# A hybrid encoder layer: output projection in 512-column products over four PSUM banks, the first half's MLP block sums kept in SBUF, and the attention mask moved from TensorE into the scan

## The chip, the cores and the metric

The kernel runs on one core of a Trainium2 chip, in one launch. The core has TensorE (products and transposes, into PSUM), VectorE, ScalarE, GpSimd and SyncE; here SyncE issues the loads from DRAM and GpSimd the stores. The metric is the device time of one execution in microseconds, as the median of several runs. One more run was recorded by the profiler, and every row below is from it.

## The reference

One layer over 2048 tokens of width 1024, in float32:

```
h    = rmsnorm(x, norm_mix_g) * (1 + sc_m) + sh_m
proj = h @ w_in                       # q, k, v, conv gates, gating MLP
z    = (q @ k.T) / 8                  # 8 heads of 64, keys s strictly before query t
w    = where(mask, exp(log_sigmoid(z) + sum over s<j<t of log_sigmoid(-z_j)), 0)
a    = w @ v
mix  = concat[a, short_gated_conv, spatial_gating] @ w_out
x    = x + g_m * mix
h    = rmsnorm(x, norm_mlp_g) * (1 + sc_f) + sh_f
x    = x + g_f * (square(relu(h @ mlp_w1)) @ mlp_w2)
out  = rmsnorm(x, final_norm_g)
```

## The kernel before

The tokens are cut into two halves of 1024, each half into two groups of 512 (`gl`), each group into four token blocks of 128 (`tb`). Every large product is made in float32r from a high and a low part of both operands, in three passes (`PASSES`): a contraction of 1024 takes eight slices of 128 times three passes, 24 instructions, into one PSUM bank. `split` makes the two parts with a ScalarE copy (L127) and a VectorE subtraction (L130).

`run` (L865) goes through four segments of blocks of units: the projections and attention of half 0 and of half 1, then the output projection of half 0 and of half 1. A unit is a piece of weights (`Unit`: loaded, split, held in `wtile`s) with a function that uses it. `bg.tick()` calls between the products step generators in the background: attention tasks, input preparation, modulation sums. The order of instructions on each engine is fixed when the kernel is built, by a list scheduler, and each engine works its own list in order.

An attention task (`attention`, L445) covers 256 queries of one head, each block of 128 against its own key block and the one before. It makes `z` with two products per block, and adds a mask of -1e38 in a third product, the identity times `mask` (L459), so that masked keys vanish. `weights` (L432) then makes log-sigmoids on ScalarE (L434 to L436), sums them backwards over keys with a scan on VectorE (L440), subtracts (L442) and exponentiates (L443). Two ticks later the weights `e` are transposed on TensorE into `wt` (L467), copied back, and one tick later multiplied with the values into `av` (L479). Keys further back are treated in `far_keys` only if a flag says so; every engine reads that flag and branches (L680, L681).

In the output projection (`out_unit`, L751) a unit holds 256 columns of `w_out`. For each pair of token blocks it loads the residual `xr`, makes 48 products of 256 columns into one bank `po` (L278, in `tok_major`), multiplies by the gate (L769, reading PSUM), adds `xr` (L771) and stores to `x1d`. While half 1 is in this segment, `prepare_input(0)` (L971) works in the background on half 0: it loads rows of `x1d`, takes squares on ScalarE, scales the rows on VectorE (L987), transposes them (L992) into banks of the common pool `pp`, and stores the result to `hd`. It then loads `hd` back, makes four block sums for a Strassen-like product with seven sub-products (L1011 to L1014) and stores them to `hs`. `inputs_after` (L1040) loads all seven inputs back (`hr`) and splits them into `h` tiles, which are shared with the projection's input `hT`, and `hx` tiles.

`Up.run` (L1073) makes 224 groups of 12 products with 512 columns into banks `pa`, `pb`, `pc`; `Down.run` (L1205) makes the second MLP product with 512 columns into banks `py`.

Of the kernel before, what the change touches and what calls it, by code (L numbers as in the profile page):

```python
# [84 lines left out]
def trunk(ctx: ExitStack, tc: tile.TileContext, x, c, ada_w, ada_b, norm_mix_g, norm_mlp_g,  # L85
# [49 lines left out]
    class Unit:  # L135


        def __init__(self, pieces):
            self.pieces, self.raw, self.w = pieces, None, None
# [10 lines left out]
        def ready(self):  # L150
            if self.w is None:
                self.fetch()
                self.w = []
                for j in range(2):
                    w = wtile()
                    split(w[:, 0], w[:, 1], self.raw[j], A)
                    w = w.rearrange("p s (k n) -> p s k n", n=UC)
                    self.w += [w[:, :, k] for k in range(KT // 2)]
            return self.w

    def unit_cols(wd, *starts):
# [8 lines left out]
        return Unit(pieces)  # L170

# [138 lines left out]
    with ExitStack() as ph:  # L310
# [86 lines left out]
        identb = ac.tile([P, P], BF16, name="identb")  # L397
        mask = ac.tile([P, 256], BF16, name="mask")
# [4 lines left out]
        def mixer_constants():  # L403

            V.tensor_copy(identb, ident)
            m32 = etile("m32")[:, :256]
            GP.memset(m32, 0.0)
            GP.affine_select(out=m32[:, P:], in_=m32[:, P:], pattern=[[-1, P]],
                             compare_op=ALU.is_gt, fill=NEG, base=0, channel_multiplier=1)
            GP.memset(m32[:, 0:P], NEG)  # L410
            V.tensor_copy(mask, m32)
# [20 lines left out]
        def weights(e, z, lo, init, save):  # L432
# [5 lines left out]
            for a, b in lo:  # L438
                r = e[:, a:b][:, ::-1]
                V.tensor_tensor_scan(r, r, r, init, ALU.add, ALU.bypass)  # L440
            V.tensor_copy(save, e.rearrange("p (b k) -> p b k", b=len(lo))[:, :, 0])
            V.tensor_tensor(e, z, e, ALU.subtract)  # L442
            A.activation(e, e, AF.Exp)  # L443

        def attention(half, pair, j, gl, qp, qq, kk, vv, a_sb):  # L445
# [5 lines left out]
            last = None  # L451
            for b in range(2):
                o = (2 * qp + b) * P
                c0 = 256 * b if first and b == 0 else 256 * b + P
                zb = z[:, b * 256:(b + 1) * 256]
# [6 lines left out]
            weights(e, z, ((0, 256), (256, G)), 0.0, carry[:, half, h, ib:ib + 2])  # L462
# [288 lines left out]
        def out_unit(half, n):  # L751
            cl = slice(n * UC, (n + 1) * UC)

            def run(gl, w):
                g = half * NG + gl
                gate = gate_bc[:, cl].unsqueeze(1).to_broadcast([P, 2, UC])
                for tb in range(0, 4, 2):
                    t0 = tb * P
                    xr = etile("xr")
                    load(out=xr.rearrange("p (b n) -> p b n", b=2),  # L760
                         in_=x2[g * G + t0:g * G + t0 + 2 * P, cl].rearrange("(b p) n -> p b n", p=P))
                    ps = bank("po")
                    for b in range(2):
                        tok_major(ps[:, b * UC:(b + 1) * UC], w, hT[gl], tb + b)
                        if half == 1:
                            bg.tick()
                            bg.tick()
                    t = etile("mo")
                    V.tensor_tensor(t.rearrange("p (b n) -> p b n", b=2),  # L769
                                    ps.rearrange("p (b n) -> p b n", b=2), gate, ALU.mult)  # L770
                    V.tensor_tensor(t, t, xr, ALU.add)  # L771
                    store(out=x1d[g][t0:t0 + 2 * P, cl].rearrange("(b p) n -> p b n", p=P),
                          in_=t.rearrange("p (b n) -> p b n", b=2))
                    bg.tick()
            return run

        def out_blocks(half):
            us = [(unit_cols(w_out2, n * UC), out_unit(half, n)) for n in range(D // UC)]
            return [us[0:2], us[2:4]]
# [85 lines left out]
        def run(seg, coming):  # L865

            for bn, blk in enumerate(blocks[seg]):
                last = bn == len(blocks[seg]) - 1
                for gl in range(NG):
# [5 lines left out]
                    for unit, use in blk:  # L875
# [8 lines left out]
                        if seg in (1, 2) and bn == 1 and gl == 0 and unit is blk[0][0]:  # L884
                            bg.drain()
                            far_keys(seg - 1, flags[seg - 1])
# [27 lines left out]
    class Up:  # L914
# [55 lines left out]

        def prepare_input(self, half):  # L971

            for g in range(NG):
                for tp in range(2):
                    xs = []
                    ss = sp.tile([P, 4], F32, name="ss", tag="ss")
                    for b in range(2):
                        t0 = (2 * tp + b) * P
                        t = landing("x")
                        load(out=t, in_=x1d[half * NG + g][t0:t0 + P, :])  # L980
                        xs.append(t)
                    yield
                    for b in range(2):
                        sum_squares(ss[:, b:b + 1], xs[b])
                    r = rstd_of(ss[:, 0:2], 2, 1.0 / D)
                    for b in range(2):
                        V.tensor_scalar_mul(xs[b], xs[b], r[:, b:b + 1])  # L987
                    yield
                    for k in range(0, KT, 2):
                        pt = bank("pt")  # L990
                        for m in range(4):
                            T.transpose(pt[:, m * P:(m + 1) * P],  # L992
                                        xs[m % 2][:, (k + m // 2) * P:(k + m // 2 + 1) * P], ident)
                        f = etile("hf")
                        for m in range(2):
                            sl = slice(m * UC, (m + 1) * UC)
                            A.activation(f[:, sl], pt[:, sl], AF.Identity,
                                         bias=SH_F[:, k + m:k + m + 1], scale=SC_F[:, k + m:k + m + 1])
                        t0 = g * G + tp * UC
                        store(out=hd[half][k:k + 2, :, t0:t0 + UC].rearrange("k p t -> p k t"),  # L1000
                              in_=f.rearrange("p (k t) -> p k t", k=2))
# [16 lines left out]
        def input(self, half, i):  # L1018

            tiles = []  # L1020
            for j in range(2):
# [10 lines left out]
                if i < 4:  # L1032
                    t = htile(2 * i + j)
                else:
                    t = self.xp.tile([P, 2, 2, G], F32R, name="hx", tag=f"hx{2 * i + j}")
                split(t[:, 0], t[:, 1], raw, A)
                tiles.append(t)
            self.h[half][i] = tiles

        def inputs_after(self, gl):  # L1040

            if gl == 0:
                bg.finish(self.coming)
                for i in (4, 5, 6, 0, 1):
                    self.input(0, i)
            else:
# [295 lines left out]
```

## Time and profile before

| | |
|---|---|
| three runs, median (lowest to highest) | 2219.91 us (2218.26 to 2220.62) |
| profiled execution: time, span of its records | 2221.83 us, 2220.1 us |
| TensorE busy; instructions | 2129.2 us (96%); 11071 |
| VectorE busy; instructions | 1445.0 us (65%); 2413 |
| ScalarE busy; instructions | 1013.7 us (46%); 1718 |
| granted TensorE clock, mean | 0.985 of full speed |
| DRAM read, written | 262.18 MB, 142.67 MB |
| stages, from the first instruction of each: attention, output projection, MLP up, MLP down | 0, 713.5, 941.8, 1600.0 us |

Busy time of TensorE counts from the start of a product to its modelled end; neighbours overlap, so a mean duration is longer than the distance between two starts, and prices of products are taken from such distances. [...]

### The profile page before, as it was taken

What the parts mean: (1) busy time and instruction counts of PE and PEld (TensorE: products, weight loads), DVE (VectorE), ACT (ScalarE), POOL (GpSimd) and SP (SyncE); (2) the same over time, 40 slices, a digit from 0 to 9 for tenths busy, and PEclk for the clock granted to TensorE, in tenths of its full rate; (3) what the DMA queues carried; (4) which work ended last, traced back from release to release, by engine and by line L of the source; (5) the groups of instructions that cost most, each with busy time, mean ns of one, the idle gap of its engine ahead of it and who ended that gap; (6) DMA issues with size and microseconds to landing.
All of it is one profiled execution on the core that took longest, in us unless ns stands there. A gap on an engine that the chain in (4) does not pass through costs nothing. (4 is left out here: it accounts for less than half of the span.)

```text
span 2220.1 us, 30066 instructions
## 1 busy us (share of the span) xinstructions
PE 2129.2 (96%) x11071; PEld 1797.7 (81%) x11071; DVE 1445.0 (65%) x2413; ACT 1013.7 (46%) x1718; POOL 332.0 (15%) x579
## 2 busy tenths in 40 slices
PE   7999999999999988899999999999999999999998
PEld 3887887888788988877888777878788888888886
DVE  4878868767768543776766777778743434347675
ACT  4645647645656234366444644444523323224432
POOL 0021211020211112223322132323200000000000
PEclk9999999999999999999999999999999999999999
DMA  8464544243435466967744687777854435437572
GB/s 304 134 207 115 163 142 131 68 140 88 117 121 162 135 224 233 327 225 244 280 156 154 225 280 256 253 237 248 308 188 153 159 120 165 143 126 231 199 241 86
DMA packets 223216, 415.37 MB, mean 187 GB/s; under 512 B 18400, under 2 KB 106416, under 8 KB 223056
## 3 DMA queue, kind: packets, MB, share of 16 engines
q1 hardware_dynamic: 177424, 264.28, 36.9%
q0 software_dynamic: 45504, 149.00, 19.3%
q8 instruction: 90, 1.47, 0.3%
q14 instruction: 70, 0.57, 0.1%
q10 hardware_dynamic: 128, 0.04, 0.0%
HBM read 262.18 MB, written 142.67 MB: 182 GB/s over the span
## 5 line engine op out<-in xcount | busy, mean ns | idle before, releaser
L1201 PE MATMUL py<-h,w 128*128 128x512 f32 x2688 | 610.7, 389 | 0.0
L1201 PEld LDWEIGHTS py<-h,w 128*128 128x128 f32 x2688 | 504.5, 188 | 105.8 <-issue 1.0
L130 DVE TENSOR_TENSOR w<-ar,w 128x1024 fp32r<-128x1024 f32 x112 | 137.1, 1224 | 263.7 <-ACT w L127 263.3
L127 ACT CAST w<-ar 128x1024 fp32r<-128x1024 f32 x112 | 118.0, 1054 | 370.4 <-PE py L1201 350.4
L127 ACT CAST w<-raw 128x512 fp32r<-128x512 f32 (+1 forms) x215 | 155.1, 736 | 131.4 <-PE pc L1089 48.9
L278 PE MATMUL po<-w,h 128*128 128x256 f32 x1536 | 195.0, 289 | 9.9 <-DVE mo L769 7.3
L130 DVE TENSOR_TENSOR w<-raw,w 128x512 fp32r<-128x512 f32 (+1 forms) x215 | 176.8, 834 | 37.9 <-ACT w L127 36.9
L278 PEld LDWEIGHTS po<-w,h 128*128 128x128 f32 x1536 | 191.4, 197 | 10.7 <-issue 10.0
L1089 PE MATMUL pc<-hx,w 128*128 128x512 f32 x768 | 193.2, 401 | 6.8 <-DVE hid L1063 6.8
L1089 PE MATMUL pa<-h,w 128*128 128x512 f32 x768 | 190.0, 396 | 7.8 <-ACT s L1056 7.8
L1089 PE MATMUL pb<-h,w 128*128 128x512 f32 x768 | 186.7, 391 | 3.6 <-DVE s L1058 3.6
L1089 PEld LDWEIGHTS pc<-hx,w 128*128 128x128 f32 x768 | 145.7, 190 | 42.6 <-DVE hid L1063 8.1
L1089 PEld LDWEIGHTS pa<-h,w 128*128 128x128 f32 x768 | 145.7, 191 | 42.4 <-ACT s L1056 11.2
L1089 PEld LDWEIGHTS pb<-h,w 128*128 128x128 f32 x768 | 143.8, 188 | 35.1 <-DVE s L1058 3.7
L269 PE MATMUL pc<-h,w 128*128 128x512 f32 x576 | 137.4, 394 | 0.0
L269 PEld LDWEIGHTS pc<-h,w 128*128 128x128 f32 x576 | 106.6, 188 | 21.3
L1064 ACT ACTIVATE hid<-hid 128x512 f32<-128x512 f32 x96 | 60.5, 630 | 124.2 <-DVE hid L1063 123.1
L278 PE MATMUL pv<-w,h 128*128 128x256 f32 x768 | 99.5, 285 | 0.0
L1300 POOL DMA_DIRECT2D out_dram<-y x24 | 13.0, 541 | 560.8 <-DVE y L1299 559.6
L1089 PE MATMUL pb<-hx,w 128*128 128x512 f32 x384 | 95.1, 396 | 1.2 <-DVE s L1058 1.2
L278 PEld LDWEIGHTS pv<-w,h 128*128 128x128 f32 x768 | 94.5, 191 | 0.1
L269 PE MATMUL pk<-h,w 128*128 128x512 f32 x384 | 94.1, 398 | 0.1
(215 smaller groups left out, 3285.3 us busy)
## 6 DMA issues: line engine op xcount, KB each, us to landing
ar<-ad SPq DMA_DIRECT2D x112, 512.0 KB, 3.9
ad<-hid POOLq DMA_DIRECT2D x128, 256.0 KB, 3.2
raw<-in_mlp_w_dram SPq DMA_DIRECT2D x62, 512.0 KB, 5.7
ad<-hsum POOLq DMA_DIRECT2D x96, 256.0 KB, 3.2
aw<-in_ada_w_dram SPq DMA_DIRECT2D x32, 512.0 KB, 4.5
f<-in_mlp_w_dram SPq DMA_DIRECT2D x32, 512.0 KB, 4.7
w2s<-f POOLq DMA_DIRECT2D x64, 256.0 KB, 2.9
w<-w2s SPq DMA_DIRECT2D x32, 512.0 KB, 4.5
```

The lines of the kernel that those rows point to most:

```text
L127: A.copy(hi, src)
L130: V.tensor_tensor(lo, src, hi.bitcast(F32), ALU.subtract)
L269: T.matmul(ps, lhsT=w[k][:, a, c0:c0 + P], rhs=hT[k][:, b], start=n == 0, stop=n == 3 * KT - 1)
L278: T.matmul(ps, lhsT=hT[k][:, a, tb * P:(tb + 1) * P], rhs=w[k][:, b], start=n == 0, stop=n == 3 * KT - 1)
L1064: A.activation(t, t, AF.Relu)
L1089: T.matmul(ps[key], lhsT=w[:, a, k * P:(k + 1) * P], rhs=h[k // 2][:, b, k % 2], start=start and m == 0, stop=m == 11, skip_group_check=no ...
L1201: T.matmul(ps[tb], lhsT=self.a[q][:, a, u * G + tb * P:u * G + (tb + 1) * P], rhs=self.w[at, c][:, b, u], start=c == 0 and u == 0 and n == ...
L1300: (load if end else store)(out=out2[t0:t0 + P, sl], in_=y)
```

## The change

- Output projection: a unit now holds 512 columns for half of the contraction (`unit_block`). `OutUnit` opens four `po` banks, one for each token block, runs 12 products of 512 columns into each with the first half of the weights, then 12 more with the second half, and after each of these the gate product, the addition and the store. `xr` is loaded one token block ahead. There is a tick after every 12 products (two or three in half 1).
- Attention: `mask`, `identb` and their products go. The scan multiplies its running value with `restart`, which is 0 on the diagonal and 1 elsewhere, so the sum begins anew there; after the subtraction a `min` with `cap` (-1e38 for masked keys, 0 elsewhere) works on the own block.
- First half's MLP inputs: `prepare_first` transposes through a bank of its own (tag `t`), keeps the four results of a column pair in SBUF, makes the sums there and splits three of them straight into `hx` tiles. Only what the other four inputs need goes through DRAM; these are loaded ahead and split later (`first_inputs`, and in `Up.run` at n = 1 and 3). There are more steps between load, squares, scaling and transposes (`rows_T`, used for half 1 too).
- The far-key branch of half 1 stands one unit earlier; inputs of half 1 load one step ahead; the first weights of the down stage follow the new places of the tiles.

```diff
             for a, b in lo:
                 r = e[:, a:b][:, ::-1]
-                V.tensor_tensor_scan(r, r, r, init, ALU.add, ALU.bypass)
+                if own is None:
+                    V.tensor_tensor_scan(r, r, r, init, ALU.add, ALU.bypass)
+                else:
+                    V.tensor_tensor_scan(r, r, restart[:, ::-1], init, ALU.add, ALU.mult)
             V.tensor_copy(save, e.rearrange("p (b k) -> p b k", b=len(lo))[:, :, 0])
             V.tensor_tensor(e, z, e, ALU.subtract)
+            if own is not None:
+                V.tensor_tensor(own, own, cap.unsqueeze(1).to_broadcast([P, 2, P]), ALU.min)
             A.activation(e, e, AF.Exp)
...
-                with tc.issue_after(last.ins) if last is not None else nullcontext():
-                    T.matmul(zb, lhsT=qq[:, 0, o:o + P], rhs=kk[:, o:o + 256], start=True, stop=False)
-                    T.matmul(zb, lhsT=qq[:, 1, o:o + P], rhs=kk[:, o:o + 256], start=False, stop=False)
-                    last = T.matmul(z[:, c0:(b + 1) * 256], lhsT=identb, rhs=mask[:, c0 - 256 * b:256],
-                                    start=False, stop=True)
+                for s in range(2):
+                    T.matmul(z[:, b * 256:(b + 1) * 256], lhsT=qq[:, s, o:o + P],
+                             rhs=kk[:, o:o + 256], start=s == 0, stop=s == 1)
...
+            def part(self, kh):
+                def run(gl, w):
+                    g = self.half * NG + gl
+                    if kh == 0:
+                        self.ps = [bank("po") for tb in range(4)]
+                    for tb in range(4):
+                        t0 = tb * P
+                        if kh == 1 or tb == 3:
+                            xr = self.xr
+                            if 4 * kh + tb < 7:
+                                t1 = g * G + (tb + 1) % 4 * P
+                                self.xr = etile("xr")
+                                load(out=self.xr, in_=x2[t1:t1 + P, self.cl])
+                        n = 12 * kh
+                        for k in range(KT // 2):
+                            for a, b in PASSES:
+                                T.matmul(self.ps[tb], lhsT=hT[gl][4 * kh + k][:, a, t0:t0 + P],
+                                         rhs=w[k][:, b], start=n == 0, stop=n == 23)
+                                n += 1
+                        if kh == 1:
+                            t = etile("mo")
+                            V.tensor_tensor(t, self.ps[tb], gate_bc[:, self.cl], ALU.mult)
+                            V.tensor_tensor(t, t, xr, ALU.add)
+                            store(out=x1d[g][t0:t0 + P, self.cl], in_=t)
+                        bg.tick()
+                        if self.half == 1:
                             bg.tick()
+                            if tb % 2:
+                                bg.tick()
...
+        def rows_T(self, half, g, tp, order, tile_, bank_):
...
+                load(out=t, in_=x1d[half * NG + g][t0:t0 + P, :])
+                xs.append(t)
+            yield None
+            yield None
+            for b in range(2):
+                sum_squares(ss[:, b:b + 1], xs[b])
+            yield None
+            r = rstd_of(ss[:, 0:2], 2, 1.0 / D)
+            for b in range(2):
+                V.tensor_scalar_mul(xs[b], xs[b], r[:, b:b + 1])
+            yield None
+            yield None
+            for k in order:
+                pt = bank_("pt")
...
+        def sums_first(self, tp, k, kept):
+            a11, a12, a21, a22 = kept[0, k], kept[0, k + 4], kept[1, k], kept[1, k + 4]
+            s1, s2, s4 = (self.xp.tile([P, G], F32, name="s", tag="s", bufs=3) for _ in range(3))
+            V.tensor_tensor(s1, a21, a22, ALU.add)
+            V.tensor_tensor(a21, a11, a21, ALU.subtract)
+            V.tensor_tensor(s2, s1, a11, ALU.subtract)
+            V.tensor_tensor(s4, a12, s2, ALU.subtract)
...
+            for i, t in ((1, s2), (3, a21), (4, s1)):
+                yield
+                o = self.h[0][i][k // 2]
+                split(o[:, 0, :, cols_], o[:, 1, :, cols_], t.rearrange("p (k t) -> p k t", k=2), A)
```

How this moves instructions shows at three places. TensorE's list where attention ends and the output projection begins, before (one tick's worth: the values' product `av` and the transposes `wt` of two older tasks, `z` of a new one):

```order
L278 MATMUL po<-w,h_7287 128x256 x6
L479 MATMUL av<-wT,vt 128x256 x2
L479 MATMUL av<-wT,vt 128x128 x4
L467 MATMUL wt<-ident,e 128x128 x4
L457 MATMUL z<-kk,qq 128x256
L458 MATMUL z<-kk,qq 128x256
L459 LDWEIGHTS identb
L459 MATMUL z<-mask,identb 128x128
L457 MATMUL z<-kk,qq 128x256
L458 MATMUL z<-kk,qq 128x256
L459 LDWEIGHTS identb
L459 MATMUL z<-mask,identb 128x128
```

and the same place after the change:

```order
L469 MATMUL z<-kk,qq 128x256 x4
L786 MATMUL po<-w,h_7224 128x512 x6
L786 MATMUL po<-w,h_7225 128x512 x6
L490 MATMUL av<-wT,vt 128x256 x2
L490 MATMUL av<-wT,vt 128x128 x4
L478 MATMUL wt<-ident,e 128x128 x4
L469 MATMUL z<-kk,qq 128x256 x4
```

The mask products are gone, and between one tick's pieces and the next stand 12 products of 512 columns in place of 48 of 256; the transposes `wt` of a task come two such groups after its `z`, here as before.

TensorE's list at the start of the output projection of half 1, before, where `pt` are the transposes of half 0's MLP input:

```order
L278 MATMUL po<-w,h_9310 128x256 x6
L278 MATMUL po<-w,h_9311 128x256 x6
L278 MATMUL po<-w,h_9312 128x256 x6
L278 MATMUL po<-w,h_9313 128x256 x6
L992 MATMUL pt<-ident,x 128x128 x12
L278 MATMUL po<-w,h_9310 128x256 x6
L278 MATMUL po<-w,h_9311 128x256 x6
L278 MATMUL po<-w,h_9312 128x256 x6
L278 MATMUL po<-w,h_9313 128x256 x6
L992 MATMUL pt<-ident,x 128x128 x4
```

and after:

```order
L786 MATMUL po<-w,h_8917 128x512 x6
L786 MATMUL po<-w,h_8918 128x512 x6
L1022 MATMUL pt<-ident,x 128x128
L786 MATMUL po<-w,h_8917 128x512
L1022 MATMUL pt<-ident,x 128x128 x3
L786 MATMUL po<-w,h_8917 128x512 x5
L1022 MATMUL pt<-ident,x 128x128 x4
L786 MATMUL po<-w,h_8918 128x512 x6
L1022 MATMUL pt<-ident,x 128x128 x4
L786 MATMUL po<-w,h_8919 128x512 x5
L1022 MATMUL pt<-ident,x 128x128 x4
```

Twelve transposes in a row have become sets of four with five or six products of 512 columns between them.

VectorE's list where the MLP's up stage ends, before (`w<-ar` are activations of the down stage, `hid<-pc` empties the last bank):

```order
L130 TENSOR_TENSOR w<-ar,w 128x1024
L1063 TENSOR_TENSOR hid<-pc,s 128x512
L1063 TENSOR_TENSOR hid<-pb,s 128x512
L130 TENSOR_TENSOR w<-ar,w 128x1024
L1070 TENSOR_TENSOR hsum<-hid 128x512
L365 TENSOR_SCALAR room<-aw,cact 128x512
L1070 TENSOR_TENSOR hsum<-hsum,hid 128x512
L1125 TENSOR_TENSOR hid<-hid 128x512
L1063 TENSOR_TENSOR hid<-pc,s 128x512
```

and after (`h_15267` and `h_15272` are weights of the down stage):

```order
L1160 TENSOR_TENSOR hid<-pc,s 128x512
L130 TENSOR_TENSOR h_15233<-w_15231,h_15233 128x1024
L1160 TENSOR_TENSOR hid<-pb,s 128x512
L130 TENSOR_TENSOR h_15238<-w_15236,h_15238 128x1024
L130 TENSOR_TENSOR w<-ar,w 128x1024
L130 TENSOR_TENSOR h_15267<-w_15265,h_15267 128x1024
L1167 TENSOR_TENSOR hsum<-hid 128x512
L130 TENSOR_TENSOR h_15272<-w_15270,h_15272 128x1024
L1167 TENSOR_TENSOR hsum<-hsum,hid 128x512
L1232 TENSOR_TENSOR hid<-hid 128x512
L1160 TENSOR_TENSOR hid<-pc,s 128x512
```

Four splits of weights now stand ahead of the last `hid<-pc`, among them two into tiles that the last products read.

## Rows read from the trace of the kernel before

**Rows 1.** Busy us (instructions) of each engine by stretch; granted clock; DMA; GB/s.

```profile
36.00:330.00 294.00, 283.62 (x1707) 242.79 (x1706) 227.22 (x451) 162.44 (x299) 41.83 (x70) 0.99 0.52 156
330.00:713.50 383.50, 368.99 (x2197) 320.67 (x2196) 277.93 (x541) 230.57 (x423) 54.89 (x91) 0.99 0.38 115
...
826.75:868.40 41.65, 34.90 (x256) 33.57 (x256) 13.73 (x32) 21.08 (x46) 11.90 (x17) 0.90 0.58 191
868.40:941.70 73.30, 65.82 (x528) 65.64 (x529) 44.42 (x58) 21.02 (x26) 18.22 (x30) 0.93 0.97 333
...
1600.00:2199.00 599.00, 599.00 (x2639) 495.04 (x2638) 304.63 (x400) 188.07 (x247) 15.71 (x29) 1.00 0.51 170
```

**Rows 2.** TensorE in order of time, one attention task: start, us, instruction.

```profile
500.08 0.36 PE L457 MATMUL z<-kk,qq 128*128 128x256 f32 x1
...
500.77 0.23 PE L459 MATMUL z<-mask,identb 128*128 128x128 bf16 x1
500.81 5.72 PE L269 MATMUL pc<-h,w 128*128 128x512 f32 x24
506.37 0.79 PE L479 MATMUL av<-wT,vt 128*128 128x256 f32 x6
...
508.11 5.72 PE L269 MATMUL pc<-h,w 128*128 128x512 f32 x24
```

**Rows 3.** TensorE in order of time, output projection; in brackets idle before, releaser.

```profile
784.05 38.04 PE L278 MATMUL po<-w,h 128*128 128x256 f32 x304 [2.33 <-PEq L681]
826.75 2.79 PE L992 MATMUL pt<-ident,x 128*128 128x128 f32 x12 [4.67 <-DVE x L987]
...
839.40 0.43 PE L992 MATMUL pt<-ident,x 128*128 128x128 f32 x2 [2.66 <-DVE x L987]
...
850.65 0.30 PE L992 MATMUL pt<-ident,x 128*128 128x128 f32 x1 [3.51 <-DVE x L987]
...
868.58 29.05 PE L278 MATMUL po<-w,h 128*128 128x256 f32 x240 [0.26 <-ACT hf L997]
904.93 37.01 PE L278 MATMUL po<-w,h 128*128 128x256 f32 x288 [7.30 <-DVE mo L769]
```

**Rows 4.** Chain of work that ended last: start, us, what; the down stage.

```profile
1686.43 512.78 PE py L1201 x2262
```

**Rows 5.** As rows 1, four stretches of 20 us of the output projection.

```profile
740.00:760.00 20.00, 20.00 (x171) 19.98 (x170) 8.24 (x14) 3.43 (x5) 2.72 (x4) 1.00 0.31 107
...
820.00:840.00 20.00, 12.67 (x87) 11.99 (x86) 9.07 (x23) 9.13 (x22) 4.28 (x6) 0.83 0.84 292
...
900.00:920.00 20.00, 15.07 (x107) 15.10 (x108) 11.43 (x15) 3.55 (x4) 4.92 (x8) 0.75 0.91 305
```

**Rows 6.** VectorE groups by line and form: busy us, mean ns; idle before.

```profile
L440 DVE TENSOR_TENSOR_SCAN e<-e 128x256 f32<-128x256 f32 x128 | 81.6, 676 | 1.2
L442 DVE TENSOR_TENSOR e<-z,e 128x512 f32<-128x512 f32 x64 | 43.9, 686 | 1.4
L437 DVE SCALAR_TENSOR_TENSOR e<-z,e 128x512 f32<-128x512 f32 x64 | 43.8, 688 | 40.1 <-ACT e L436 39.8
...
L560 DVE TENSOR_TENSOR vt<-pv,vt 128x256 fp32r<-128x256 f32 x32 | 13.4, 418 | 8.4 <-ACT vt L559 8.0
```

**Rows 7.** One task: TensorE's next product after `z`, ScalarE's last step on `e`.

```profile
721.07 5.99 PE L278 MATMUL po<-w,h 128*128 128x256 f32 x48
...
730.17 0.63 ACT L443 ACTIVATE e<-e 128x512 f32<-128x512 f32 x1 [3.00 <-DVE e L442]
```

**Rows 8.** VectorE and ScalarE in order of time, ahead of the 7.30 us.

```profile
885.90 0.69 DVE L1012 TENSOR_TENSOR hs<-hs,a 128x512 f32<-128x512 f32 x1 [3.21 <-DMA hs<-hs]
...
903.90 1.04 ACT L127 CAST hx<-hr 128x1024 fp32r<-128x1024 f32 x1 [11.77 <-DMA hr<-hs]
```

**Rows 9.** MLP up: one wait of TensorE, and VectorE's last copy out of `pc`.

```profile
1275.44 3.01 PE L1089 MATMUL pa<-h,w 128*128 128x512 f32 x12 [1.42 <-ACT s L1056]
...
1601.81 0.68 DVE L1063 TENSOR_TENSOR hid<-pc,s 128x512 f32<-128x512 f32 x1
```

More of the change, by code (lines that the diff above doesn't have):

```diff
@@ L1 @@
-from contextlib import ExitStack, nullcontext
+from contextlib import ExitStack
 import concourse.bass as bass
@@ L430, in trunk, with weights @@
             V.memset(t, 0.0)
-        def weights(e, z, lo, init, save):
+        def weights(e, z, lo, init, save, own=None):
             A.activation(e, z, AF.Abs)
@@ L749, in phase1_blocks @@
             ]
[L751 to L765, printed above, removed]
-                            bg.tick()
[L767 to L775, printed above, removed]
@@ L781, in trunk @@
+        def out_blocks(half):
+            blks = []
+            for cb in range(2):
+                out = OutUnit(half, cb)
+                blks.append([(unit_block(w_out2, 4 * kh, cb * G), out.part(kh)) for kh in range(2)])
+            return blks
         class Ahead:
@@ new lines, in put_rows, with place @@
+        def put_rows(self, half, g, tp, k, f):
+            t0 = g * G + tp * UC
+            store(out=hd[half][k:k + 2, :, t0:t0 + UC].rearrange("k p t -> p k t"),
+                  in_=f.rearrange("p (k t) -> p k t", k=2))
+        DIRECT = (1, 3, 4)
+        def place(self, i):
+            if i in self.DIRECT:
+                n = 2 * self.DIRECT.index(i)
+                return [self.xp.tile([P, 2, 2, G], F32R, name="hx", tag=f"hx{n + j}")
+                        for j in range(2)]
+            n = 2 * (0, 2, 5, 6).index(i)
+            return [htile(n + j) for j in range(2)]
@@ new lines, in prepare_first @@
+        def prepare_first(self):
+            for i in self.DIRECT:
+                self.h[0][i] = self.place(i)
+            for tp in range(2):
+                kept = {}
+                for g in range(NG):
+                    order = (0, 4, 2, 6) if g else (0, 2, 4, 6)
+                    for got in self.rows_T(0, g, tp, order, lambda: self.out_tile("hf"),
+                                           lambda name: self.pabc.tile([P, G], F32, name=name, tag="t")):
+                        if got is not None:
+                            k, f = got
+                            kept[g, k] = f
+                            if g == 0 or k >= 4:
+                                self.put_rows(0, g, tp, k, f)
+                            if g == 1 and k >= 4:
+                                yield
+                                yield from self.sums_first(tp, k - 4, kept)
+                        yield
@@ L974, in prepare_input @@
                 for tp in range(2):
[L975 to L1001, printed above, removed]
+                    for got in self.rows_T(half, g, tp, range(0, KT, 2), lambda: etile("hf"),
+                                           bank):
+                        if got is not None:
+                            self.put_rows(half, g, tp, *got)
                         yield
@@ L1016, in prepare_input, with input_load @@
                     store(out=hs[half][j][k], in_=e[j])
-        def input(self, half, i):
-            tiles = []
+        def input_load(self, half, i):
+            raws = []
             for j in range(2):
```

114 lines of the change are left out of this document (77 added, 37 removed).

## The prediction

> **What bounds the kernel now.** I read the view by stretches first, cut where the stages begin: attention and projections to 713.5 us, output projection to 941.7, MLP up to 1600, MLP down to the end. TensorE is busy for 283.6 of 294.0 us and for 369.0 of 383.5 in the two attention stretches, all of 599.0 in the down stage, but for only 34.9 of 41.65 and 65.8 of 73.3 in the last two stretches of the output projection [rows 1]. So TensorE's own work counts almost everywhere, and its waits count in the output projection. I then read TensorE's rows in order of time. In the output projection stand four waits for VectorE's scaling of `x` (L987) and for its product (L769): 4.67, 2.66, 3.51 and 7.30 us, with one of 2.33 us for the branch [rows 3]. [...] VectorE, busy 505.2 of 677.5 us in attention [rows 1], is the engine that could take over.
>
> **The change part by part.**
>
> *Mask products leave TensorE.* Each attention task issues six instructions for `z`; from the first (500.08) to the next product's start (500.81) is 0.73 us [rows 2]. Four 128x256 products alone, at the 0.121 us of the output projection (29.05 us for 240) [rows 3], take 0.48. The difference, 0.25 us, is the two mask products with the change of operand type around them; 64 tasks make 16 us. Lower bound: the two mask starts themselves are followed after 0.04 us (500.77 to 500.81) [rows 2], so if all else of the 0.25 belongs to the transposes ahead of the task, 128 starts make 5 us. TensorE is 96% busy there, so I take this as path: **-16 us**.
>
> *The mask moves to VectorE.* The scan gets a second operand and a multiply, and each task one `min` over 256 columns. For the `min` the nearest row is a 128x256 tensor-tensor, 418 ns [rows 6]; 64 make 27 us of VectorE time. For the scan I bound: nothing, since it already has a second operation slot and a two-operation row, 688 ns for 512 columns, is no slower than plain tensor-tensors of that size (686 ns) [rows 6]; or the feedback paid once more, 676 - 418 = 258 ns, giving 934 ns and 33 us over 128 scans [rows 6]. I take nothing, because the 688 ns row is the like case. With the `min` alone VectorE is busy about 532 of some 662 us, 80% against 75%. The cover is what stands between a task's `z` and its transposes: two products of 5.56 us (500.81 to 506.37) and small pieces of 1.74 (to 508.11) [rows 2], 12.9 us, 12.6 without a mask. Of a `z` that ends at 721.07 the weights are ready 9.7 us later (730.17 plus 0.63) [rows 7]. Those 3 us of slack absorb 0.4 where VectorE is not queued up. The attention stretches hold 10.4 + 14.5 = 25 us without TensorE work [rows 1], mostly waits of under 1 us for VectorE; I let them grow by an eighth: **+3 us** (0 to 24). On VectorE, behind the `min`, stand the copies out of PSUM; TensorE waits for them through the banks.
>
> [...]
>
> *512-column products.* 1536 products of 128x256 become 768 of 128x512. At 0.121 us the first cost 185.9 us. The like product, token-major with 512 columns, is the down stage's: 512.78 us for 2262, 0.2267 each [rows 4]; 768 cost 174.1. **-11.8 us.** Bounds: the 304 products from 784.05 take 0.125 us each [rows 3], which would make it -18; the undisturbed stretch from 740 has 171 in 20 us, 0.117 each [rows 5], which makes it -5.6. I take the long undisturbed run between them.
>
> [...]
>
> *Waits for the scaling of `x`.* The new generator steps twice between load and squares, once before the scaling and twice before the transposes, where the old one stepped once and once; at five steps per 48 old products (5.8 us) that is three steps, some 3.5 us, more room. Waits of 4.67, 2.66 and 3.51 [rows 3] then shrink to about 1.2, 0 and 0; since the transposes now share a single PSUM bank, a fresh cause of waits, I keep 2 us of 10.8: **-9 us**.
>
> *The last 7.30 us* [rows 3]. VectorE reached L769 late because its queue held sums waiting for stores (`hs<-hs`, 3.21 us once) while ScalarE waited 11.77 us for the reload [rows 8], in a stretch that moved 333 GB/s with the DMA engines 97% busy [rows 1]. The change keeps the sums in SBUF: four `S4` stores and no `S1` to `S3` traffic for this half, eight fewer loads of `hd` of 512 KB, four fewer `hd` stores of 256 KB, twelve fewer `hs` stores of 256 KB and six fewer `hs` loads of 512 KB: 11 MB of the 24.4 MB (73.3 us at 333 GB/s). What is late next are the `xr` loads, asked for one block (2.7 us) ahead; four banks let TensorE run 8 us on before it needs the first one back. **-7.3 us.**
>
> *Clock.* In the two slow stretches 87 instructions take 12.67 us busy and 107 take 15.07 [rows 5]; at the 0.117 of the stretch from 740 the first, which mixes in transposes, would be 2.5 us shorter, and at 0.121 the second 2.1. With the waits gone: **-4.5 us**.
>
> *A new wait at the start of the stage.* Steps of attention tasks used to stand 48 products of 256 columns apart; now 12 of 512, 2.7 us, and the rows of the order show three transposes with only two such groups and their own 1.5 us pieces between them and their `z`: 8.4 us, against 9.7 + 0.4 needed [rows 7]. Three times 1.7 us, with part of it taken up by the wait before: **+4 us** (0 to 10), and **+1** for the clock. The far-key branch moves ahead by one unit; its 2.33 us stay.
>
> *MLP up.* Inputs load one step ahead, which touches waits such as the 1.42 us at 1275.44, where ScalarE came late to its copy behind an input's split [rows 9]; two or three of these make -3. At the end, the last weight tiles now reuse the slots of the last two inputs, so VectorE splits them between the last product and the copy out of bank `pc`, which stood at 1601.81, 1.8 us after the down stage began [rows 9]; two splits and three sums more push it some 4 us, and the fourth bank of the down stage waits about 2 us: **-1 us** together (-6 to +4).
>
> The sum is -16 + 3 - 11.8 - 9 - 7.3 - 4.5 + 5 - 1 = -41.6 us. The profiled execution took 2221.83 us (span 2220.1), 1.9 above the median of the runs, so 2180 for it and about **2178 us** as a median.
>
> **Rivals.**
> - *VectorE takes over in attention.* If the scan pays the feedback twice, VectorE gains 27 + 33 us in 662 and is 85% busy on average and near full between 100 and 300 us. The 25 us of gaps would about double: 2178 - 3 + 24 = 2199 us. For it: VectorE is already the releaser of most gaps. Against: the two-operation row [rows 6].
> - *The output projection gives back.* If the attention tail costs 10 and the transposes, each of which now needs the one bank back from ScalarE, keep the old waits with their clock, the stage saves 14 us less: 2192 us. For it: the waits are TensorE's queue order, set ahead of time. Against: the rows of the order put products between the transposes.
> - *Slower: the task's chain is exposed.* If all of 0.418 + 2 x 0.258 = 0.93 us reaches TensorE in each of 64 tasks, 60 us come in place of 3: 2235 us. It decides from about 0.77 us exposed per task (41.6 + 3 + 4.4 us over 64). Against: 3 us of slack per task and 172 us of VectorE idle time in the stage.
> - *More than forecast.* Shorter steps let attention waits vanish too: 2152 us.
> - *Nothing*: gains given back in the DMA-bound up stage, 2220 us; against it, TensorE is 100% busy in the down stage, so time gained ahead of it is kept.
>
> **How the numbers follow.** Forecast 0.64, VectorE 0.12, output projection 0.13, more 0.05, nothing 0.03, slower 0.03. A measurement of this kernel tells about 0.2%, 4.4 us, from no change: faster 0.94, same 0.03, slower 0.03. The likeliest case alone runs from 2166 to 2190 by its bounds; the range takes in both neighbours: 2160 to 2203.
>
> **What would show it.** The mask group gone and `z` tasks of 0.5 us; scans at 676 ns and a `min` near 418; 768 products at 0.227; the stage from the first `po` to the first `pa` near 200 us, not 228.2; waits of 1 to 3 us at three transposes right after its start, none of 7 before its last quarter; a granted clock of 0.97 or more in its stretches. Scans above 800 ns, or attention stretches that are not at least 8 us shorter, would prove the forecast wrong.

## The result and the profile after

The changed kernel takes 2184.41 us as a median (2183.62 to 2191.97), the kernel before 2219.09 us on the same chip: ratio 0.9852, 95% interval 0.9828 to 0.9875. That is 34.7 us less where 41.6 were forecast (2178 us), and inside the range. The profiled execution took 2184.64 us, 37.2 us less than the one of before.

The view by stretches of both kernels, cut at the first instruction of each stage (columns as in [rows 1]); before:

```profile
36.00:713.50 677.50, 652.61 (x3903) 563.46 (x3902) 505.15 (x992) 393.01 (x722) 96.72 (x161) 0.99 0.44 133
713.50:941.77 228.27, 207.05 (x1662) 204.99 (x1661) 121.06 (x192) 77.14 (x130) 44.15 (x66) 0.95 0.70 232
941.77:1600.00 658.23, 636.74 (x2754) 514.17 (x2753) 484.64 (x757) 336.91 (x582) 174.75 (x317) 0.99 0.68 237
1600.00:2220.10 620.10, 611.43 (x2693) 504.99 (x2691) 316.56 (x436) 192.59 (x263) 15.71 (x29) 0.99 0.51 167
```

and after:

```profile
36.00:706.40 670.40, 636.86 (x3775) 551.28 (x3773) 522.36 (x1046) 391.70 (x719) 96.21 (x158) 0.99 0.44 135
706.40:905.36 198.96, 193.26 (x889) 156.78 (x888) 125.92 (x209) 81.07 (x141) 30.56 (x51) 0.99 0.63 211
905.36:1558.53 653.17, 633.61 (x2754) 512.59 (x2753) 478.20 (x750) 332.92 (x577) 174.84 (x317) 0.99 0.68 236
1558.53:2182.90 624.37, 611.98 (x2693) 504.84 (x2691) 320.49 (x440) 195.06 (x267) 16.00 (x29) 1.00 0.51 168
```

The reader takes the first two numbers of each row, the length and TensorE's busy time; their difference is its idle time. Attention lost 15.8 us of work but only 7.1 us of length: idle time rose from 24.9 to 33.5 us. The output projection went from 228.3 to 199.0 us, idle time there from 21.2 to 5.7. The up stage is 5.1 us shorter and the down stage 4.3 us longer.

The groups by line that answer to [rows 6]: the scan with its second operand, and the new `min`.

```profile
L453 DVE TENSOR_TENSOR_SCAN e<-e,restart 128x256 f32<-128x256 f32 x128 | 81.4, 675 | 1.1
L457 DVE TENSOR_TENSOR e<-e,cap 128x256 f32<-128x256 f32 x64 | 26.8, 419 | 1.1
```

The scan's multiply costs nothing (675 against 676 ns), and the `min` is priced like its neighbour in [rows 6] (419 against 418 ns). A scan of 256 columns takes 675 ns, about as long as a subtraction of 512 (686 ns, [rows 6]).

TensorE's waits in the output projection, in order of time, answer to [rows 3]:

```profile
712.05 0.38 PE L490 MATMUL av<-wT,vt 128*128 128x256 f32 x1 [2.71 <-ACT wT L127]
713.09 1.08 PE L490 MATMUL av<-wT,vt 128*128 128x256 f32 x5 [0.65 <-DVE wT L130]
...
720.69 0.66 PE L478 MATMUL wt<-ident,e 128*128 128x128 f32 x4 [0.40 <-ACT e L458]
...
769.26 5.95 PE L786 MATMUL po<-w,h 128*128 128x512 f32 x25 [0.32 <-PEq L692]
...
816.09 0.33 PE L1022 MATMUL pt<-ident,x 128*128 128x128 f32 x1 [0.76 <-DVE x L1016]
...
829.96 0.30 PE L1022 MATMUL pt<-ident,x 128*128 128x128 f32 x1 [0.22 <-DVE x L1016]
```

The four large waits are gone. New ones stand behind the first twelve products, of about the size forecast but mostly at another instruction: the transposes `wt`, which were to wait for the weights `e`, wait 0.40 us (and 0.20 at 728.81), while 2.71 and 0.65 us stand at `av`, for the two parts of `wT`. The transposes before it end at 706.08; ScalarE copies `wT` 5.3 us later, behind splits of `h` and `w`:

```profile
704.81 1.12 ACT L127 CAST h<-ct 128x512 fp32r<-128x512 f32 x2
705.84 1.05 ACT L127 CAST w<-raw 128x1024 fp32r<-128x1024 f32 x1
706.79 2.18 ACT L127 CAST h<-ct 128x512 fp32r<-128x512 f32 x4
...
711.41 0.59 ACT L127 CAST wT<-wt 128x512 fp32r<-128x512 f32 x1
```

The stretches that answer to [rows 5]:

```profile
706.40:726.00 19.60, 15.84 (x81) 13.27 (x80) 19.48 (x36) 15.37 (x28) 1.08 (x2) 0.91 0.58 189
740.00:760.00 20.00, 20.00 (x91) 16.43 (x90) 6.90 (x11) 2.11 (x2) 2.17 (x4) 1.00 0.36 108
780.00:800.00 20.00, 20.00 (x90) 16.53 (x89) 10.41 (x15) 5.33 (x8) 2.17 (x4) 1.00 0.59 197
820.00:840.00 20.00, 19.60 (x96) 15.22 (x96) 11.74 (x23) 11.54 (x25) 5.82 (x9) 1.00 0.68 229
...
880.00:900.00 20.00, 20.00 (x90) 16.58 (x89) 13.13 (x19) 6.38 (x8) 1.98 (x4) 1.00 0.74 252
```

Only the first of them is below full clock (0.91, the others 1.00). The products stand 20 us / 90 = 0.222 us apart, a little under the 0.227 of the forecast.

In the MLP, VectorE and TensorE in order of time show a new long wait of the up stage and the start of the down stage:

```profile
1055.01 0.69 DVE L1100 TENSOR_TENSOR hs<-a,a 128x512 f32<-128x512 f32 x1 [6.19 <-DMA a<-hd]
...
1062.97 5.49 PE L1186 MATMUL pb<-hx,w 128*128 128x512 f32 x12 [5.79 <-DVE s L1155]
...
1558.53 4.24 PE L1308 MATMUL py<-h,w 128*128 128x512 f32 x18
...
1563.82 0.68 DVE L1160 TENSOR_TENSOR hid<-pc,s 128x512 f32<-128x512 f32 x1
...
1564.56 12.99 PE L1308 MATMUL py<-h,w 128*128 128x512 f32 x56 [1.79 <-DVE hid L1160]
```

VectorE stood 6.2 us for the reload of the second half's rows, and the copy that TensorE needed was behind it in its list. VectorE's last copy out of `pc` starts 5.3 us after the down stage began (1.8 before [rows 9]).

### The profile page after: what moved, and what is told of

Same layout as the page of the kernel before. It is cut to its first block, busy times and chain, and to the rows that moved or that the text cites. A ratio compares the mean times of both kernels' runs of the same rounds, so it can differ in the third digit from the quotient of the medians.

```text
span 2182.9 us, 28254 instructions
## 1 busy us (share of the span) xinstructions
PE 2095.7 (96%) x10175; PEld 1735.6 (80%) x10175; DVE 1464.8 (67%) x2481; ACT 1014.6 (46%) x1724; POOL 319.2 (15%) x564
## 5 line engine op out<-in xcount | busy, mean ns | idle before, releaser
L1186 PE MATMUL pb<-hx,w 128*128 128x512 f32 x768 | 192.9, 400 | 7.9 <-DVE s L1155 7.9
L786 PE MATMUL po<-w,h 128*128 128x512 f32 x768 | 181.8, 394 | 0.3 <-PEq L692 0.3
L1186 PEld LDWEIGHTS pb<-hx,w 128*128 128x128 f32 x768 | 145.1, 190 | 43.8 <-DVE s L1155 9.6
L786 PEld LDWEIGHTS po<-w,h 128*128 128x128 f32 x768 | 142.9, 189 | 29.5 <-issue 0.7
L278 PE MATMUL pc<-h,w 128*128 128x512 f32 x576 | 135.5, 391 | 0.0
L1186 PE MATMUL pb<-h,w 128*128 128x512 f32 x384 | 93.5, 392 | 3.3 <-DVE s L1155 3.3
L1186 PE MATMUL pc<-hx,w 128*128 128x512 f32 x384 | 95.1, 396 | 0.0
L1186 PE MATMUL pc<-h,w 128*128 128x512 f32 x384 | 92.9, 391 | 1.7 <-DVE hid L1160 1.7
```

What stands on the lines that cost most here:

```text
L278: T.matmul(ps, lhsT=w[k][:, a, c0:c0 + P], rhs=hT[k][:, b], start=n == 0, stop=n == 3 * KT - 1)
L786: T.matmul(self.ps[tb], lhsT=hT[gl][4 * kh + k][:, a, t0:t0 + P], rhs=w[k][:, b], start=n == 0, stop=n == 23)
L1186: T.matmul(ps[key], lhsT=w[:, a, k * P:(k + 1) * P], rhs=h[k // 2][:, b, k % 2], start=start and m == 0, stop=m == 11, skip_group_check=no ...
```

## The experiments

Indented text is what was expected, written before the run. Each ratio is to the kernel before on the same chip, with a 95% interval; stages come from one profiled execution.

**Which part gave what: attention alone, all but attention, output projection alone.** `e1_mask` is the kernel before with the diff's hunks on `restart`, `cap`, `weights` and `attention` and no other; `e3_nomask` is the changed kernel without these hunks.

> The kernel before with the attention part of the change alone (mask in the scan and the min). Reading of the trace after the change: in the attention stage TensorE's busy time fell by 17 us but its idle time grew by 10, so the first product of the output projection came only 7 us earlier. If that loss belongs to the attention edit itself, this run shows the first po product near 706.5 us, the output projection still at 228 us, and some 2212 us in all (7 us faster than before). If the loss comes from the other edits (the output weights, fetched during attention in another form), first po near 701 us and some 2206 us.

> The changed kernel with the attention part undone (mask products back on TensorE, no min). If the parts add up: first po product near 713.5 us as before, the output projection 199 us long as after, and 2191 us in all, 28 us faster than before. If the output projection's gain needed the shorter attention tasks (they run behind its first products), the stage takes 203 us or more and the time is 2196 us or above.

`e1_mask` took 2210.71 us, ratio 0.9964 (0.9938 to 0.999); `e3_nomask` 2192.44 us, 0.9875 (0.9852 to 0.9898). In e3 the first `po` is back at 713.4 and the output projection takes 198.1, so its gain does not need the attention edit: the first-named outcome held. In e1 it held for the time and the idle time, 31.9 us, so the loss belongs to the attention edit. Its first `po` comes at 711.4 us, though, 2.1 us earlier than before and not 7 (output projection 226.9). Most of the 11.3 us by which e1's profile is shorter lies in the up stage, whose code it leaves alone:

```profile
711.37:938.22 226.85, 205.46 (x1658) 203.01 (x1656) 124.40 (x199) 78.95 (x133) 44.25 (x66) 0.96 0.70 234
938.22:1588.77 650.55, 631.20 (x2754) 509.14 (x2753) 484.89 (x757) 337.64 (x582) 175.08 (x317) 1.00 0.70 239
```

So the time of e1 says little about attention.

`e6_out` takes from the change only `unit_block`, `OutUnit` and the branch's place:

```diff
-                        pt = bank("pt")
+                        pt = (bank("pt") if half else
+                              self.pabc.tile([P, G], F32, name="pt", tag="t"))
```

> The kernel before with the new output projection alone (512-column products, four banks, weights by half of the contraction, far-key branch one unit earlier); the mask stays on TensorE and the MLP input is prepared as before, except that its transposes use the single bank of their own, as after. Theory of the forecast: the waits for the scaling of x (10.8 us) and the 7.3 us behind the sums belong to the preparation of the input, and only the products get shorter: the stage from the first po to the first pa takes 211 to 216 us, the whole 2203 to 2208 us. Rival: the longer run of four banks hides these waits whatever the preparation does: the stage takes 203 us or less, 2195 us.

2217.36 us, ratio 0.9983 (0.9969 to 0.9997). The stage took 224.4 us, longer than either theory said. Its row by stretches, then TensorE and VectorE of `e6_out` in order of time:

```profile
714.22:938.58 224.36, 199.09 (x895) 159.28 (x894) 121.53 (x192) 78.72 (x131) 38.59 (x66) 0.94 0.68 235
...
846.59 0.30 PE L1019 MATMUL pt<-ident,x 128*128 128x128 f32 x1 [1.00 <-DVE x L1013]
...
887.68 7.16 PE L784 MATMUL po<-w,h 128*128 128x512 f32 x18 [18.96 <-DVE mo L789]
...
875.05 0.69 DVE L1038 TENSOR_TENSOR hs<-a,a 128x512 f32<-128x512 f32 x1 [13.40 <-DMA a<-hd]
...
882.88 0.69 DVE L1039 TENSOR_TENSOR hs<-hs,a 128x512 f32<-128x512 f32 x1 [3.90 <-DMA hs<-hs]
...
886.93 0.69 DVE L789 TENSOR_TENSOR mo<-po,gate_bc 128x512 f32<-128x512 f32 x1 [1.30 <-DMA hs<-hs]
```

The waits for `x` are two of 1 us, though the preparation has its old steps here: the new output projection, or the transposes through a bank of their own, hides these, as the rival said of them. But VectorE then stands 13.4 us for the reload of `hd` and 3.9 for a store, the gate product behind them comes late, and TensorE's last wait grew from 7.3 to 19 us. Busy time fell from 207.05 to 199.1 us, at a granted clock of 0.94 against 0.95.

**Spacing in the preparation of rows.** `e7_yields`, the changed kernel with

```diff
             yield None
-            yield None
             for b in range(2):
                 sum_squares(ss[:, b:b + 1], xs[b])
-            yield None
             r = rstd_of(ss[:, 0:2], 2, 1.0 / D)
...
                 V.tensor_scalar_mul(xs[b], xs[b], r[:, b:b + 1])
-            yield None
             yield None
```

> The changed kernel with the old spacing in the preparation of rows: one step between load and squares, none before the scaling, one before the transposes (three steps fewer). Theory: this spacing is what removed the waits for x; 5 us or more of waits at the transposes come back, the stage takes 204 us or more, 2189 us or more. Rival: the lighter DMA traffic and the sums in SBUF removed them: the stage stays within 1.5 us of 199, the time within 2182 to 2187 us.

2198.69 us, ratio 0.9883 (0.9859 to 0.9907); the stage takes 207.3 us, 8.3 more. (The profile is 14.4 us longer in all; 4.2 of that are attention and 1.9 the up stage, with unchanged code.) TensorE's waits came back, beside these one of 1.09 us for `x`; behind them ScalarE ahead of the first:

```profile
825.82 0.66 PE L1019 MATMUL pt<-ident,x 128*128 128x128 f32 x4 [3.62 <-ACT hf L1024]
...
854.55 0.45 PE L1019 MATMUL pt<-ident,x 128*128 128x128 f32 x1 [3.10 <-DVE x L1014]
...
822.90 1.06 ACT L216 ACTIVATE junk<-x 128x1024 bf16<-128x1024 f32 x1 [2.89 <-DMA x<-x]
...
824.75 1.02 ACT L1024 ACTIVATE hf<-pt,cols 128x256 f32<-128x256 f32 x2
```

The theory held: beside the sums on chip, the three steps are worth 8 us. The wait of 3.62 us is one for the transposes' bank: ScalarE's copy out of it stood behind squares that waited 2.89 us for the load of `x`. Why the same old steps cost 7.8 us of waits here and 2 us in `e6_out` stays open. With e6, and since e3 shows that the attention edit matters little here, the stage goes from 228.3 us to 224.4 (512-column products and the transposes' bank), 207.3 (the new preparation without its steps) and 199.0 (all).

**What keeps attention from its gain: more and less of the `min`.** `e4_min2` has the line with `ALU.min` twice. `e5_scanonly` has none; the scan masks by itself:

```diff
-                    V.tensor_tensor_scan(r, r, restart[:, ::-1], init, ALU.add, ALU.mult)
+                    V.tensor_tensor_scan(r, restart[:, ::-1], r, -NEG, ALU.mult, ALU.add)
```

with the zeros of `restart` one column earlier, so that the state is 1e38 down to the diagonal and begins anew behind it.

> The changed kernel with each min issued twice (the second changes nothing): 64 more VectorE instructions of 419 ns, 27 us of VectorE time. Theory, VectorE's queue: the min delays the copies and splits behind it, and the first dose already costs some 8 us of TensorE idle; the second costs at least as much: first po near 715 us, 2193 us or more. Rival, less cover: TensorE waits more only because its own work between a task's steps got shorter, VectorE has room: at most 2 us more, 2186 us.

> The changed kernel without the min: the scan multiplies its running state by the restart row and adds the next value, starting from 1e38, so the masked keys get 1e38 out of the scan itself; the same function is computed. Theory, VectorE's queue: 27 us of VectorE time less gives back most of the 8 to 10 us of TensorE idle: first po near 699 us, 2176 us. Rival, less cover: first po stays within 2 us of 706.4 and the time within 2182 to 2186 us. If the form mult-add of the scan is slower than 675 ns, its row shows it.

2196.56 us, ratio 0.9899 (0.9872 to 0.9925), for two; 2184.58 us, 0.9836 (0.9814 to 0.9859), for none, its scan at 677 ns. The stretch from 36 us to the first `po` in the two:

```profile
36.00:714.87 678.87, 641.32 (x3779) 555.15 (x3777) 544.75 (x1107) 391.38 (x719) 96.08 (x158) 0.98 0.44 133
```

```profile
36.00:706.34 670.34, 638.54 (x3772) 554.74 (x3771) 501.58 (x987) 392.24 (x720) 95.82 (x158) 0.98 0.44 134
```

Taken singly the two contradict each other: the second `min` costs 8.5 us of length, taking out the first gives nothing. But one profile is not enough here: the same attention code stands in five runs (after, e7, e8, e9, e11), and this stretch takes 670.4, 674.6, 671.6, 673.8 and 675.6 us. So I compare groups: mask on TensorE (before, e3, e6) mean 677.7 us, busy 652.8, idle 24.8; one `min` (the five) 673.2, 640.8, 32.4; no `min` (e5, and the last two runs below) 668.7, 637.1, 31.6; two 678.9, 641.3, 37.6. By length a `min` of 27 us VectorE time is worth some 5 us here (4.5 the first, 5.7 the second, from one run). But of the first's 4.5 only 0.8 us is idle time; the other 3.7 is busy time, which in the five runs of one code goes from 636.9 to 644.2 us, so this price is not shown. The larger part of the idle time is the rival's: without any `min`, 15.7 us of products leave and 6.8 us of idle time come. The waits of `av` on `a_sb` are 0.8 us in the kernel before, 6.1 with the `min` and 3.6 in each run without it, where one of 3.2 us on `wT` has come.

**The order of VectorE's list.** `e10_order`:

```diff
-                        getattr(self, what)(ps, gl, ct)
                         bg.tick()
+                        getattr(self, what)(ps, gl, ct)
```

> The changed kernel with the steps of the attention tasks issued ahead of the convolution's own work on a finished bank and not behind it: TensorE's order stays nearly as it is, VectorE's copy of av and the split of wT come ahead of some 3 us of convolution work. What is still open in attention: TensorE's idle time grew by 8 us and neither more nor less min accounts for it. Theory, order of VectorE's queue: TensorE, relieved of the mask, reaches the same places earlier, where the copy that frees av stands behind convolution work and weight splits; the four waits on a_sb (6.1 us) shrink to 2 us or less and first po comes 3 to 5 us earlier than in the other kernels with this attention (706 to 711 us). Rival, chain length: a task's own chain is what is late, the waits only change their name (wT, e, kk), and first po stays within 706 to 711 us.

2190.77 us, ratio 0.9869 (0.9842 to 0.9896); first `po` at 706.8 us. TensorE's waits from 36 to 706 us by line and releaser (total, times, longest), after and `e10_order`:

```profile
PE av L490 <- DVE a_sb L495: 6.1, 4, 2.0
PE wt L478 <- DVE wT L130: 5.5, 7, 1.6
...
PE z L469 <- DVE kk L538: 2.3, 2, 1.4
```

```profile
PE z L469 <- DVE kk L538: 8.7, 2, 4.4
PE wt L478 <- DVE wT L130: 5.5, 7, 1.7
...
PE av L490 <- DVE a_sb L495: 1.5, 2, 1.2
```

The wait on `a_sb` fell as the theory said, and `z` waited for `kk` by more than that: idle time is 34.1 us against 33.5. The waits change their name, as the rival said.

**Three waits of after, one place each.** `e8_down` puts the second half's first four inputs back into the slots that the down weights take next, loads them in an order that fits, and splits the first down weights earlier; shown is this last part:

```diff
...
-                if last in (0, 2, 5, 6):
-                    c = 2 * (0, 2, 5, 6).index(last)
-                    down.weights(0, c)
-                    down.weights(0, c + 1)
+                if 0 < last <= 4:
+                    down.weights(0, 2 * last - 2)
+                    down.weights(0, 2 * last - 1)
```

`e9_reload` has four `yield`s in place of two behind the loads of `hd` in `prepare_input`. `e11_ticks`:

```diff
-                        bg.tick()
+                        if self.half == 1 or tb % 2:
+                            bg.tick()
```

> The changed kernel with the second half's inputs in the old slots (its first four in the slots that the weights of the down stage take next, its last three in the others), loaded in an order that fits, and the first eight weight tiles of the down stage split during four products before the last, as before. Theory: the 4.3 us by which the down stage got longer (620.1 to 624.4) come from weight tiles that wait for the last two inputs: the stage is back within 1 us of 620, the whole near 2180 us. Rival: they come from elsewhere and stay: 624, 2184 us.

> The changed kernel with four steps in place of two between the reload of the second half's transposed rows and the sums over them. In the profile after, VectorE stood 6.2 us at such a sum for its reload and TensorE then 5.8 us for a copy queued behind it. Theory: two more products of room (5.4 us) take nearly all of this wait: the up stage is 4 to 6 us shorter, the whole 2179 us. Rival: the reload itself comes later by as much, since it queues behind stores, or another wait takes the place: up stage and time unchanged within 2 us.

> The changed kernel with the steps of the attention tasks in the first half of the output projection 24 products of 512 columns apart and not 12. Theory: the 4 us of waits at the start of the stage (2.71, 0.65, 0.40, 0.20 us) come from steps that stand too close; they vanish, the stage takes 195 to 196 us, the whole some 2181 us. Rival: the tail then runs into the far-key branch, ahead of which it must end, and the waits move there: the stage stays at 198 to 200 us.

- `e8_down`: down stage 620.7 us, 3.7 less, as the theory said; 2184.6 us, ratio 0.9838 (0.9811 to 0.9865), so the whole shows nothing above its noise.
- `e9_reload`: the wait of 5.79 us became 2.87, and one of 3.87 stands elsewhere; up stage 651.4 us, 1.8 less, 2185.48 us (0.9832, 0.981 to 0.9854). Inconclusive: this stage takes 653 to 658 us in the other runs with the same code.
- `e11_ticks`: output projection 194.7 us, 4.2 less, the waits of 2.71 and 0.40 gone, that of 0.65 still there; 2181.32 us (0.9823, 0.9797 to 0.985). The theory held for the stage.

**Together.** `e12_all` is `e5_scanonly` with the edits of e8 and e9, `e13_best` that with the edit of e11.

> The changed kernel with three edits together: the scan that masks by itself without a min, the second half's inputs in the old slots (down stage 3.7 us shorter alone), and four steps ahead of the sums over the reload (up stage 1.8 us shorter alone). If they add up: first po near 706 us, out stage 198, up 651, down 620.5: span near 2176 us, some 6 us below the changed kernel. Rival: the up stage gives it back, since its waits follow the DMA traffic: 2182 us or more.

> The kernel of the run with three edits (scan that masks by itself, old slots for the second half, four steps ahead of the reload's sums), and with the steps of the attention tasks 24 products apart at the start of the output projection as well. If the wider steps add to the rest: out stage 195 us in place of 198.6, the others as there, 2174 to 2176 us as a median. If the 4 us are given back in the up stage, whose waits follow the DMA traffic: 2178 to 2180 us.

`e12_all`: 2178.57 us, ratio 0.9814 (0.9792 to 0.9837): the edits add up to some 6 us, as expected, with an interval that still overlaps the changed kernel's. `e13_best`: 2173.63 us (2168.88 to 2178.27), ratio 0.9792 (0.9771 to 0.9813), which lies clear of the changed kernel's interval and meets the first-named outcome. Its stages:

```profile
36.00:703.48 667.48, 637.43 (x3773) 553.11 (x3772) 501.21 (x987) 391.92 (x720) 95.83 (x158) 0.98 0.44 135
703.48:896.69 193.21, 191.09 (x889) 155.30 (x888) 124.16 (x204) 80.19 (x140) 30.46 (x51) 1.00 0.65 217
896.69:1550.90 654.21, 635.10 (x2754) 512.94 (x2752) 482.36 (x754) 334.90 (x580) 175.00 (x318) 0.99 0.69 238
1550.90:2171.80 620.90, 611.36 (x2693) 505.16 (x2691) 316.41 (x435) 192.64 (x263) 15.14 (x28) 0.99 0.51 166
```

The up stage takes 654.2 us here and 649.7 in `e12_all`, with the same code, against 653.2 in the changed kernel, so what the edit of e9 brings is not shown. The gain of `e13_best` lies in the other three stages.

## Why the prediction was right, and where it was not

By stage, in the profiles, attention gave 7.1 us where 13 were forecast, the output projection 29.3 for 27.6 and the MLP 0.8 for 1.

- *Mask products leave TensorE, -16.* Right in size: busy time falls by 15.8 us in the profiles; by the groups above, by 15.7 without a `min` and 12 with it, a difference within the spread of the five runs.
- *The mask moves to VectorE, +3.* This is the term that failed, within its bounds of 0 to 24. The prices were right (675 and 419 ns), the growth of the waits was not. The step was "I let them grow by an eighth"; idle time grew by three tenths, 7.6 us on the mean of five (24.8 to 32.4) in place of 3. Of these, 6.8 come without any `min`. Attention became 7.1 us shorter in the profile and 4.5 on the mean of five, below the 8 that the prediction set as its own test. "TensorE is 96% busy there, so I take this as path" was too simple. What the 6.8 us are is settled in part: not the `min`, and not the place of the convolution's work in VectorE's list (`e10_order`). That a task's own chain keeps its length while TensorE reaches each step sooner fits the runs, but is argued: without a `min` the chain has the steps of before, with a scan of 677 ns for 676, and a shorter one was not tried.
- *512-column products, -11.8.* In `e6_out`, where the granted clock was 0.94, busy time of the stage fell by 8 us; where the products of 256 columns run alone at a clock of 1.00, the kernel before has 211 in the 25 us from 870, 0.1185 us each, and after has 0.222: 1536 and 768 of them give -11.5, near the forecast. The lower bound of -5.6 was too low, since 17 of the 171 instructions in the stretch from 740 are other ones.
- *Waits for `x`, -9.* Right in size: of 10.8 us some 1 is left. The cause named, the three steps, is not all of it: without them `e7_yields` costs 8.3 us, but in `e6_out` the old steps leave only 2 us of waits.
- *The last 7.30 us.* Right, and worth more than forecast: `e6_out` shows that with the sums through DRAM the faster products run into a wait of 19 us, which is gone in `e7_yields`, where the sums stay in SBUF.
- *Clock, -4.5.* The two slow stretches of the forecast are those at 0.83 and 0.75 in [rows 5]. From `e6_out` to after, busy time falls by another 5.8 us at a granted clock of 0.99 in place of 0.94, near the forecast.
- *New wait at the start, +4.* Right in size, 2.71 + 0.65 + 0.40 + 0.20 us, and in that the steps stand too close: `e11_ticks` gives back 4.2. The place was wrong: only 0.60 us is the transposes' wait for `e` that was worked out; 3.36 us are waits for `wT`, one step further on, so the sum met by luck. The far-key branch, said to stay at 2.33 us, took 0.32.
- *MLP up, -1 together.* The sum came out (-0.8 in the profiles), in part by luck: its end was dearer, 4.3 us in the down stage in place of 2, shown by `e8_down`, and the 5.1 us gained in the up stage lie within its spread (650.6 us in e1 and 658.2 before, with the same code there).

Of the rivals, "VectorE takes over" fell with the scan's 675 ns and "the output projection gives back" with a stage of 199 us. "The task's chain is exposed" has the right direction at a far smaller size: 7.6 us of idle time over 64 tasks are 0.12 us a task, not 0.93. "Nothing" took the up stage for DMA-bound; in the profile of before TensorE is busy for 636.74 of its 658.23 us, at a DMA share of 0.68. The miss of 7 us is attention's.

## What to carry to other kernels

Work taken from the busiest engine need not count in full: here 15.7 us left and 6.8 us of idle time came, so read idle time before and after, not the busy share. A faster loop should be changed together with the transfer that it will run into: the 512-column products alone shortened the stage by 4 us, with the sums on chip by 21, and with more steps in the preparation by 29. An operation that exists only to mask can be put into a recurrence's initial value and restart; the scan takes no longer for it (677 against 676 ns).

## What was not expected of the hardware

- After TensorE's wait of 19 us in `e6_out` the clock stayed low beyond the wait. The view by stretches, around the wait and behind it:

```profile
870.00:890.00 20.00, 2.32 (x6) 1.84 (x7) 7.36 (x12) 2.09 (x2) 4.71 (x9) 0.57 0.92 342
890.00:910.00 20.00, 17.79 (x62) 13.37 (x61) 14.21 (x19) 2.10 (x2) 6.72 (x13) 0.83 0.91 322
```

  In the second, 62 instructions take 17.79 us, 0.287 each, where the undisturbed stretch of after has 0.222: 4 us on top of the wait.
- The scan takes the same time in its three forms: add alone 676, add then multiply 675, multiply then add 677 ns.
- One program's stages vary from run to run by more than single edits bring: in the five runs with the same attention code TensorE's busy time from 36 us to the first `po` goes from 636.9 to 644.2 us, the length from 670.4 to 675.6, with idle times of 31.4 to 33.5. Small edits were therefore read from waits and from groups of runs.
